# One transformer block on one core: gates and branch projections with features on partitions

## The chip, the cores and the metric

The kernel runs on one core of a Trainium2 chip, in one launch. The metric is device time in microseconds (us) from start to end of an execution. TensorE (PE) multiplies, VectorE (DVE) and ScalarE (ACT) do the elementwise work, GpSimd (POOL) does a little, and nearly all transfers from memory are issued by SyncE (SP).

## What is computed

One block of a hybrid model for 256 tokens of width 1024. The part that the change touches, cut from the reference:

```python
proj = jnp.einsum('bsd,de->bse', h, w_in[l])
qa, ka, va, qb, kb, vb, gate_logits = jnp.split(proj, splits, axis=-1)
oa = moba_attention(to_heads(qa, 8), to_heads(ka, 8), to_heads(va, 8), rel_bias)
ob = stick_breaking_attention(to_heads(qb, 8), to_heads(kb, 8), to_heads(vb, 8))
ya = jnp.einsum('bse,ed->bsd', merge_heads(oa), w_br_moba[l])     # 512 -> 1024
yb = jnp.einsum('bse,ed->bsd', merge_heads(ob), w_br_sb[l])       # 512 -> 1024
gates = jax.nn.sigmoid(gate_logits)
g_a, g_b = jnp.split(gates, 2, axis=-1)
mixed = jnp.einsum('bsd,de->bse', g_a * ya + g_b * yb, w_out[l])  # 1024 -> 1024
x = x + gt_m[:, None, :] * mixed
```

Ahead of it stand the modulation vectors and a norm, behind it a second norm, a gated feed-forward part with a short convolution (`up`, `down`) and the last norm.

## The kernel before

All products are made from two halves: a value is split into a rounded part (`wh`, `zh`, ..., a cast on ACT) and the rest (`wl`, `zl`, ..., a subtraction on DVE), and each product is three matmuls (high by high, low by high, high by low). `split` does this for weights, 1024 columns at a time, `hilo` for activations.

A `Stage` is one projection onto 512 output features. Its contraction is cut into units of two blocks of 128 rows. There are two ways to run a unit. In the token form (`Stream.mm`, line 164) 128 tokens are the stationary operand, 512 columns of weights move, and the output bank holds tokens on partitions; a unit is six matmuls of 128x512 for each of the two token tiles. In the feature form (`mm_fm`, line 252) 128 weight columns are the stationary operand, all 256 tokens move, and the output holds features on partitions; a unit is 24 matmuls of 128x256 in two halves. `qkb` and most of `up` use the feature form, the others the token form.

The order of stages is `gate0`, `gate1`, `qkb0`, `qkb2`, `vb`, `gate2`, `gate3`, then `ya0`, `ya1`, `yb0`, `yb1` (the branch projections), `out0`, `out1`, `up`, `down`. `together` runs a unit for both token tiles in turn; `staggered` runs token tile 1 some units behind token tile 0. While `gate0` to `ya1` run, generators add the attention of eight head pairs (`moba_pair`, then `stick_pair`; four pairs each) and the modulation vectors: `ada_part` loads pieces of 128x1024 into a pool of two buffers and accumulates them on DVE (`acc_gtm`, `acc_shf`, `acc_scf`, line 700). From these programs a scheduler with priorities makes one fixed sequence for each engine; each engine then goes through its sequence in order and waits at semaphores. PSUM banks of the stages come from a pool of three (`mm`), weight parts from pools of six (`wh`, `wl`), raw weights from a pool of three.

The gates: `gate_put` applies tanh to the bank (ACT, lines 759 to 764; for the second branch a copy first, and tanh in place when all heads are done) and keeps the result in an SBUF tile of 128x2048, tokens on partitions. `ya_put` multiplies one plus the gate by the bank (DVE, line 822). `yb_put` does the same for the second gate (line 829), adds (line 830), transposes the sum with four matmuls against the identity into a bank `zt` (line 838), and splits `zt` into `zh` and `zl` (lines 147, 148), the stationary operands of `out`. When the last of the four is made, the loads of `x` for the residual are issued (line 834).

## Time and profile before

| | us |
|---|---|
| median of 3 runs | 433.92 (433.38 to 434.75) |
| the profiled execution | 434.69 |
| its span, first to last instruction | 433.0 |
| PE busy | 410.1 (95%) |
| DVE busy | 335.6 (77%) |
| ACT busy | 254.0 (59%) |

The profile is of one execution. Times in it count from the start of the span. The mean granted TensorE clock was 0.982 of full speed. Matmuls overlap, so the pace of a stream of them is read from starts, not from the length of one.

### The profile page before, as it was taken

To read this page: it belongs to the slowest core of one execution; us is meant where nothing else is said; L and a number is where in the kernel's file an instruction comes from. 1 tells how busy PE (TensorE), PEld (TensorE's weight loads), DVE (VectorE), ACT (ScalarE), POOL (GpSimd) and SP (SyncE) were. 2 spreads that over 40 slices of the span, in tenths; PEclk is the share of its full clock that TensorE was granted. 3 is DMA by queue.
4 is the path that set the end of the run, shared out by engine and by line. 5 is a ranking of instruction groups with operands and counts; after the bars stand their busy time and mean duration, and the time that the engine had idled before them with its cause. 6 is when DMAs were issued, how large, how long until landed. Compare 5 with 4: busy or idle time off the path is not lost.

```text
span 433.0 us, 6769 instructions
## 1 busy us (share of the span) xinstructions
PE 410.1 (95%) x2598; PEld 364.4 (84%) x2598; DVE 335.6 (77%) x509; ACT 254.0 (59%) x397; POOL 41.4 (10%) x76
## 2 busy tenths in 40 slices
PE   7899889999799899999996999999999999999993
PEld 7898887789698688788884899999999999888882
DVE  3789969689689977996858779999998888546333
ACT  3244537867966779942446758666776666433312
POOL 3624430000001010000041000000000000000001
PEclk9999969999999999999999999999999999999997
DMA  8999987988467556577537487677576655473102
GB/s 260 323 325 332 290 287 259 323 292 289 147 239 254 188 203 234 197 244 288 177 115 242 155 277 251 202 254 247 178 226 175 183 193 195 149 266 122 47 0 97
DMA packets 67128, 94.44 MB, mean 218 GB/s; under 512 B 2558, under 2 KB 45697, under 8 KB 67096
## 3 DMA queue, kind: packets, MB, share of 16 engines
q1 hardware_dynamic: 65943, 90.77, 63.6%
q0 software_dynamic: 576, 1.67, 1.2%
q10 hardware_dynamic: 576, 1.57, 1.0%
q8 instruction: 20, 0.33, 0.3%
q14 instruction: 13, 0.10, 0.1%
HBM read 92.94 MB, written 1.06 MB: 217 GB/s over the span
## 4 chain that ended last, share of the span: by engine, by line
PE 61%; DVE 13%; ACT 9%; DMA 8%; issue 4%; SPq 1%; POOL 1%; POOLq 0%; DVEq 0%; ACTq 0%
PE ps_up L252 26%; PE ps_down L164 14%; DVE acc L385 4%; PE ps_out L164 4%; DMA ada_gtm<-in_w_ada_dram 3%; PE ps_yb L164 3%; PE ps_ya L164 3%; PE ps_qkb L252 3%; DMA raw_wA<-in_w_in_dram 2%; PE ps_up L164 2%; DMA ada<-in_w_ada_dram 2%; PE pA L406 1%; DMA ada_shf<-in_w_ada_dram 1%; DVE wl_gate L139 1%; SPq L365 1%
## 5 line engine op out<-in xcount | busy, mean ns | idle before, releaser
L138 ACT CAST wh_up<-raw_up 128x1024 fp32r<-128x1024 f32 x44 | 46.1, 1050 | 27.7 <-PE ps_up L252 21.9
L252 PE MATMUL ps_up<-h2h__2313,wh_up 128*128 128x256 f32 x320 | 58.0, 283 | 0.0
L252 PE MATMUL ps_up<-h2h__2313,wl_up 128*128 128x256 f32 x320 | 57.9, 283 | 0.0
L139 DVE TENSOR_TENSOR wl_up<-raw_up,wh_up 128x1024 fp32r<-128x1024 f32 x42 | 51.1, 1220 | 8.5 <-ACT wh_up L138 8.3
L252 PE MATMUL ps_up<-h2l__2314,wh_up 128*128 128x256 f32 x320 | 57.1, 279 | 0.0
L252 PEld LDWEIGHTS ps_up<-h2h__2313,wl_up 128*128 128x128 f32 x320 | 46.9, 191 | 0.0
L139 DVE TENSOR_TENSOR wl_down<-raw_down,wh_down 128x1024 fp32r<-128x1024 f32 x22 | 26.9, 1224 | 25.6 <-ACT wh_down L138 25.6
L252 PEld LDWEIGHTS ps_up<-h2l__2314,wh_up 128*128 128x128 f32 x320 | 46.6, 190 | 0.0
L252 PEld LDWEIGHTS ps_up<-h2h__2313,wh_up 128*128 128x128 f32 x320 | 46.4, 189 | 0.2
L138 ACT CAST wh_down<-raw_down 128x1024 fp32r<-128x1024 f32 x22 | 23.2, 1053 | 32.2 <-PE ps_down L164 23.6
L941 DVE SCALAR_TENSOR_TENSOR cv<-ps_up,wc,cv 128x255 f32<-128x255 f32 (+1 forms) x80 | 34.4, 476 | 1.4 <-ACT cv L935 0.9
L164 PE MATMUL ps_down<-wl_down,hh_a 128*128 128x512 f32 x88 | 34.9, 397 | 0.0
L164 PE MATMUL ps_down<-wh_down,hh_a 128*128 128x512 f32 x88 | 34.7, 395 | 0.0
L164 PE MATMUL ps_down<-wh_down,hl_a 128*128 128x512 f32 x88 | 34.7, 394 | 0.0
L164 PE MATMUL ps_gate<-wh_gate,hh 128*128 128x512 f32 x64 | 26.2, 409 | 1.9 <-DVE vbl L145 1.5
L385 DVE SCALAR_TENSOR_TENSOR acc<-ada,ca,acc 128x256 f32<-128x256 f32 (+1 forms) x43 | 24.7, 576 | 1.5
L164 PE MATMUL ps_gate<-wl_gate,hh 128*128 128x512 f32 x64 | 25.4, 396 | 0.0
L164 PE MATMUL ps_gate<-wh_gate,hl 128*128 128x512 f32 x64 | 25.3, 396 | 0.0
L935 ACT ACTIVATE cv<-ps_up,vc,wc 128x256 f32<-128x256 f32 x40 | 20.5, 562 | 5.7 <-PE ps_up L252 5.7
L139 DVE TENSOR_TENSOR wl_gate<-raw_gate,wh_gate 128x1024 fp32r<-128x1024 f32 x16 | 20.3, 1286 | 3.2 <-ACT wh_gate L138 3.2
L478 ACT CAST whA<-raw_wA 128x1024 fp32r<-128x1024 f32 (+1 forms) x9 | 8.6, 958 | 22.9 <-DMA raw_wA<-in_w_in_dram 22.9
L164 PEld LDWEIGHTS ps_down<-wh_down,hh_a 128*128 128x128 f32 x88 | 16.5, 188 | 4.1
(268 smaller groups left out, 930.7 us busy)
## 6 DMA issues: line engine op xcount, KB each, us to landing
raw_up<-in_w_up_dram SPq DMA_DIRECT2D x44, 512.0 KB, 5.0
raw_down<-in_w_down_dram SPq DMA_DIRECT2D x10, 1024.0 KB, 5.0
ada<-in_w_ada_dram SPq DMA_DIRECT2D x16, 512.0 KB, 7.5
raw_gate<-in_w_in_dram SPq DMA_DIRECT2D x8, 1024.0 KB, 7.2
raw_wA<-in_w_in_dram SPq DMA_DIRECT2D x8, 768.0 KB, 9.0
raw_qkb<-in_w_in_dram SPq DMA_DIRECT2D x8, 512.0 KB, 5.7
ada_gtm<-in_w_ada_dram SPq DMA_DIRECT2D x8, 512.0 KB, 5.4
ada_shf<-in_w_ada_dram SPq DMA_DIRECT2D x8, 512.0 KB, 5.7
```

Of the source, the lines that this page charges most:

```text
L138: nc.scalar.copy(wh[:, :n], t[:, a:a + n])
L139: (lo or nc.vector).tensor_sub(wl[:, :n], t[:, a:a + n], wh[:, :n].bitcast(F32))
L164: nc.tensor.matmul(ps, sx(k)[:, sl], w[:, c0:c0 + n], start=first and i == 0, stop=last and i == 2)
L252: nc.tensor.matmul(st.ps[f // 2][:, f % 2 * S:(f % 2 + 1) * S], wi[:, kk * 512 + f * P:kk * 512 + (f + 1) * P], sx(k0 + kk), start=first a ...
L365: nc.sync.dma_start(raw[:, i * D:(i + 1) * D].rearrange("p (k f) -> p k f", f=P), w_ada[:, i * D + j * P:i * D + (j + 1) * P].rearrange("( ...
L385: nc.vector.scalar_tensor_tensor(a, wk[:, parts, k, :], ca[:, k:k + 1], a, op0=ALU.mult, op1=ALU.add)
L406: nc.tensor.matmul(psqk[f // 2][:, f % 2 * S:(f % 2 + 1) * S], wp[0][n == 2][:, f * P:(f + 1) * P], (hh, hl, hh)[n][:, j, :], start=j == 0 ...
L478: nc.scalar.copy(wh[i][:, a:a + n], wws[j][:, i * 1024 + a:i * 1024 + a + n])
L935: nc.scalar.activation(ct[:, b, :], tp[:, b * S:(b + 1) * S], AF.Identity, bias=bconv[:, fb:fb + 1], scale=wc[:, 88 + fb:89 + fb])
L941: nc.vector.scalar_tensor_tensor(ct[:, b, d:], tp[:, b * S:(b + 1) * S - d], wc[:, (2 - d) * 44 + fb:(2 - d) * 44 + fb + 1], ct[:, b, d:], ...
```

## The change

The four gate stages and the four branch stages run in the feature form. The gate tiles therefore hold features on partitions, 8 blocks of 128 features by 256 tokens, and so do the products with the branch projections. Their sum has the layout that `zh` and `zl` need, so it is split straight from the gate tile in SBUF, and the 16 transposes and their banks are left out. `yb` runs `together`, and no longer staggered by six units. The loads of `x` are issued behind the `yb` stages.

```diff
+    def blocks(i, half):
+        return slice(4 * i + 2 * half, 4 * i + 2 * half + 2)
 ...
-                gates[g] = att.tile([P, NT, D], F32, tag=("ga", "gc")[g], name=f"gate{g}")
-            gt = gates[g][:, t, i % 2 * 512:(i % 2 + 1) * 512]
+                gates[g] = att.tile([P, KT, S], F32, tag=("ga", "gc")[g], name=f"gate{g}")
+            gt = gates[g][:, blocks(i % 2, half), :].rearrange("p a b -> p (a b)")
 ...
-        return Stage(f"gate{i}", KT, columns(w_in, GA + i * 512), tiles(hh), tiles(hl), gate_put(i))
+        return Stage(f"gate{i}", KT, columns(w_in, GA + i * 512), tiles(hh), tiles(hl), gate_put(i), fm=True)
 ...
+    def gated(g, i, half, ps):
+        gt = gates[g][:, blocks(i, half), :]
+        nc.vector.scalar_tensor_tensor(gt, gt, 1.0, ps.rearrange("p (a b) -> p a b", a=2), op0=ALU.add, op1=ALU.mult)
+        return gt
 ...
-            g0, g1 = (gates[g][:, t, i * 512:(i + 1) * 512] for g in range(2))
-            nc.vector.scalar_tensor_tensor(g1, g1, 1.0, ps, op0=ALU.add, op1=ALU.mult)
+            half, ps = ps
+            g1, g0 = gated(1, i, half, ps), gates[0][:, blocks(i, half), :]
             nc.vector.tensor_add(g0, g0, g1)
 ...
-                    nc.sync.dma_start(xr[tt], x[tt * P:(tt + 1) * P, :])
-            yield 3
-            tp = bank(sm, f"zt{t}{i}")
-            for a in range(4):
-                nc.tensor.transpose(tp[:, a * P:(a + 1) * P], g0[:, a * P:(a + 1) * P], ident)
-            s4 = slice(4 * i, 4 * i + 4)
-            tsl = slice(t * P, (t + 1) * P)
-            hilo(zh[:, s4, tsl], zl[:, s4, tsl], tp.rearrange("p (a b) -> p a b", a=4), 0.5)
+            hilo(zh[:, blocks(i, half), :], zl[:, blocks(i, half), :], g0, 0.5)
+            yield 1
 ...
-    staggered([u for us in y_units[2:] for u in us], 6)
+    together([u for us in y_units[2:] for u in us])
+    for t in range(NT):
+        nc.sync.dma_start(xr[t], x[t * P:(t + 1) * P, :])
```

The `ya` and `yb` stages get `fm=True` too. The scheduler also orders work around these stages in another way, at three places above all.

DVE during `gate1` and `qkb0` (stretch 97 to 108 us of the profile), before: `acc_gtm` are the pieces of a modulation vector, `wl_qkb` weight halves, `pl` the low half of the second head pair's probabilities, which the products `po_m` need.

```order
111 L700 SCALAR_TENSOR_TENSOR acc_gtm<-ada_gtm_1048,ca,acc_gtm 128x1024
112 L139 TENSOR_TENSOR wl_qkb_0_1195<-raw_qkb_0_969,wh_qkb_0_1194 128x1024
113 L616 RECIPROCAL su_1058<-su_1058 128x4
114 L139 TENSOR_TENSOR wl_qkb_2_1250<-raw_qkb_0_969,wh_qkb_2_1249 128x1024
115 L145 TENSOR_TENSOR oa_771<-po_m_1071,oa_770 64x256
116 L632 TENSOR_TENSOR pl_1101<-pt_1102,ph_1100 128x384
117 L632 TENSOR_TENSOR pl_1101<-pt_1107,ph_1100 128x384
118 L145 TENSOR_TENSOR oa_771<-po_m_1071,oa_770 64x256
119 L700 SCALAR_TENSOR_TENSOR acc_gtm<-ada_gtm_1129,ca,acc_gtm 128x1024
```

The same stretch of DVE now:

```order
111 L700 SCALAR_TENSOR_TENSOR acc_gtm<-ada_gtm_1138,ca,acc_gtm 128x1024
112 L700 SCALAR_TENSOR_TENSOR acc_gtm<-ada_gtm_1225,ca,acc_gtm 128x1024
113 L616 RECIPROCAL su_1148<-su_1148 128x4
114 L139 TENSOR_TENSOR wl_qkb_0_1291<-raw_qkb_0_1029,wh_qkb_0_1290 128x1024
115 L145 TENSOR_TENSOR oa_771<-po_m_1167,oa_770 64x256 x2
116 L700 SCALAR_TENSOR_TENSOR acc_gtm<-ada_gtm_1274,ca,acc_gtm 128x1024
117 L632 TENSOR_TENSOR pl_1197<-pt_1198,ph_1196 128x384
118 L632 TENSOR_TENSOR pl_1197<-pt_1203,ph_1196 128x384
119 L139 TENSOR_TENSOR wl_qkb_2_1346<-raw_qkb_0_1029,wh_qkb_2_1345 128x1024
```

The last two pieces of `acc_gtm`, which wait for transfers, moved ahead: one of them now stands directly in front of `pl`.

DVE at the start of `gate2` (stretch 135 to 144 us), before: `acc_shf` are pieces of the next modulation vector.

```order
157 L145 TENSOR_TENSOR qk_1477<-ps_qkb_1_1316,qk_1477 128x512
158 L139 TENSOR_TENSOR wl_gate_2_1629<-raw_gate_0_1346,wh_gate_2_1628 128x1024
159 L700 SCALAR_TENSOR_TENSOR acc_shf<-ada_shf_1558,ca,acc_shf 128x1024
160 L700 SCALAR_TENSOR_TENSOR acc_shf<-ada_shf_1602,ca,acc_shf 128x1024
161 L659 SCALAR_TENSOR_TENSOR t_1562<-zs_1530,t_1562 128x768
```

DVE at the start of `gate2` now:

```order
157 L145 TENSOR_TENSOR qk_1573<-ps_qkb_1_1412,qk_1573 128x512
158 L700 SCALAR_TENSOR_TENSOR acc_shf<-ada_shf_1654,ca,acc_shf 128x1024
159 L139 TENSOR_TENSOR wl_gate_2_1725<-raw_gate_0_1442,wh_gate_2_1724 128x1024
160 L700 SCALAR_TENSOR_TENSOR acc_shf<-ada_shf_1698,ca,acc_shf 128x1024
161 L659 SCALAR_TENSOR_TENSOR t_1658<-zs_1626,t_1658 128x768
```

One piece of `acc_shf` moved ahead of a weight half; the last transfer for that vector is issued when this piece is done.

DVE at the end of `yb` (stretch 197 to 210 us), before:

```order
222 L830 TENSOR_TENSOR gate_905<-gate_905,gate_1807 128x512
223 L829 SCALAR_TENSOR_TENSOR gate_1807<-gate_1807,ps_yb_0_2100 128x512
224 L830 TENSOR_TENSOR gate_905<-gate_905,gate_1807 128x512
225 L139 TENSOR_TENSOR wl_out_4_2170<-raw_out_4_2043,wh_out_4_2169 128x1024
226 L148 SCALAR_TENSOR_TENSOR zl<-zt_2128,zh 128x4x128
227 L829 SCALAR_TENSOR_TENSOR gate_1807<-gate_1807,ps_yb_1_2121 128x512
228 L139 TENSOR_TENSOR wl_out_6_2188<-raw_out_4_2043,wh_out_6_2187 128x1024
```

DVE at the end of `yb` now:

```order
224 L826 SCALAR_TENSOR_TENSOR gate_1945<-gate_1945,ps_yb_1_2317 128x512
225 L139 TENSOR_TENSOR wl_out_6_2463<-raw_out_4_2271,wh_out_6_2462 128x1024
226 L148 SCALAR_TENSOR_TENSOR zl<-gate_947,zh 128x512
227 L839 TENSOR_TENSOR gate_947<-gate_947,gate_1945 128x512
228 L139 TENSOR_TENSOR wl_out_0_2476<-raw_out_0_2345,wh_out_0_2475 128x1024
229 L148 SCALAR_TENSOR_TENSOR zl<-gate_947,zh 128x512
230 L826 SCALAR_TENSOR_TENSOR gate_1945<-gate_1945,ps_yb_0_2385 128x512
231 L826 SCALAR_TENSOR_TENSOR gate_1945<-gate_1945,ps_yb_1_2398 128x512
232 L839 TENSOR_TENSOR gate_947<-gate_947,gate_1945 128x512 x2
233 L139 TENSOR_TENSOR wl_out_2_2486<-raw_out_0_2345,wh_out_2_2485 128x1024
234 L148 SCALAR_TENSOR_TENSOR zl<-gate_947,zh 128x512 x2
```

The last two sums (row 232) come behind two weight halves of `out`, and the last two `zl` behind a third.

## Rows read from the trace of the kernel before

**Rows 1.** The page, part 1: busy us (share of the span), instructions.

```profile
PE 410.1 (95%) x2598; PEld 364.4 (84%) x2598; DVE 335.6 (77%) x509; ACT 254.0 (59%) x397; POOL 41.4 (10%) x76
```

**Rows 2.** Waits of PE, 60 to 250 us: total us, times, longest.

```profile
PE ps_qkb L252 <- DVE qk L148: 2.4, 1, 2.4
PE ps_gate L164 <- DVE vbl L145: 1.5, 1, 1.5
PE cu L668 <- DVE lkl L663: 1.0, 1, 1.0
```

**Rows 3.** Stretches (us): busy (instructions) of PE, PEld, DVE, ACT, POOL; clock; DMA.

```profile
98.00:110.00 12.00, 12.00 (x105) 11.68 (x104) 11.16 (x22) 8.82 (x25) 0.00 (x0) 1.00 0.78 260
110.00:123.00 13.00, 10.61 (x67) 8.84 (x68) 9.26 (x14) 9.84 (x18) 0.00 (x0) 0.87 0.49 162
160.00:175.00 15.00, 14.04 (x70) 11.58 (x70) 12.17 (x16) 13.68 (x20) 1.05 (x2) 1.00 0.52 176
193.00:207.00 14.00, 14.00 (x74) 11.72 (x73) 10.52 (x16) 5.31 (x6) 0.54 (x1) 1.00 0.64 227
```

**Rows 4.** The chain that ended last: start us, us, what.

```profile
180.92 5.60 PE ps_ya L164 x24
205.18 0.44 PE zt L838 x4
260.29 54.22 PE ps_up L252 x456
```

**Rows 5.** PE in order of time: start us, us, what, and idle before.

```profile
104.47 0.39 PE L575 MATMUL po_m<-ph,vah 128*128 128x512 f32 x1
116.10 0.51 PE L252 MATMUL ps_qkb<-hh,wh_qkb 128*128 128x256 f32 x2 [2.39 <-DVE qk L148]
```

**Rows 6.** DVE in order of time, 101 to 145 us, same columns.

```profile
101.51 1.00 DVE L632 TENSOR_TENSOR pl<-pt,ph 128x384 fp32r<-128x384 f32 x2
103.00 1.28 DVE L700 SCALAR_TENSOR_TENSOR acc_gtm<-ada_gtm,ca,acc_gtm 128x1024 f32<-128x1024 f32 x1
107.75 0.16 DVE L611 TENSOR_SCALAR mx<-mx 128x4 f32<-128x4 f32 x1
114.22 1.22 DVE L139 TENSOR_TENSOR wl_vb<-raw_vb,wh_vb 128x1024 fp32r<-128x1024 f32 x1 [0.59 <-ACT wh_vb L138]
115.36 0.68 DVE L148 SCALAR_TENSOR_TENSOR qk<-ps_qkb,qk 128x512 fp32r<-128x512 f32 x1
144.13 1.28 DVE L700 SCALAR_TENSOR_TENSOR acc_shf<-ada_shf,ca,acc_shf 128x1024 f32<-128x1024 f32 x1 [0.43 <-DMA ada_shf<-in_w_ada_dram]
```

**Rows 7.** ACT in order of time, 107 to 115 us.

```profile
107.95 0.51 ACT L614 ACTIVATE sb<-sb,mx 128x256 f32<-128x256 f32 x1 [3.11 <-DVE mx L611]
114.08 0.61 ACT L147 ACTIVATE qk<-ps_qkb 128x512 fp32r<-128x512 f32 x1
```

**Rows 8.** SP's queue in order of time, and the landing of `ada_gtm` transfers.

```profile
94.91 3.48 SPq L706 DMA_DIRECT2D ada_gtm<-in_w_ada_dram  x2
...
DMA to landing us min/median/max: 4.7/5.4/6.0
```

**Rows 9.** One of the stretches after the wait at 113.7: PE busy, clock, DMA.

```profile
118.00:119.00 1.00, 1.00 (x5) 0.50 0.00 0
```

**Rows 10.** ACT and DVE at the end of `yb`, in order of time.

```profile
201.99 1.05 ACT L138 CAST wh_out<-raw_out 128x1024 fp32r<-128x1024 f32 x1 [7.72 <-PE ps_yb L164]
...
204.82 0.68 DVE L829 SCALAR_TENSOR_TENSOR gate<-gate,ps_yb 128x512 f32<-128x512 f32 x1
205.41 1.22 DVE L139 TENSOR_TENSOR wl_out<-raw_out,wh_out 128x1024 fp32r<-128x1024 f32 x1
206.55 0.68 DVE L830 TENSOR_TENSOR gate<-gate,gate 128x512 f32<-128x512 f32 x1
```

**Rows 11.** Groups by line, 55 to 250 us: busy us, mean ns.

```profile
L148 DVE SCALAR_TENSOR_TENSOR zl<-zt,zh 128x512 fp32r<-128x512 f32 x4 | 2.7, 686 | 0.9 <-ACT zh L147 0.9
L145 DVE TENSOR_TENSOR h2l__2314<-h2f,h2h__2313 128x512 fp32r<-128x512 f32 x4 | 2.7, 688 | 0.4 <-ACT h2h__2313 L144 0.3
```

More of the change, by code (lines that the diff above doesn't have):

```diff
@@ L817, in block_kernel @@
     zl = slot("hl", [P, KT, S], F32R, "zl")
+    def gated(g, i, half, ps):
+        gt = gates[g][:, blocks(i, half), :]
+        nc.vector.scalar_tensor_tensor(gt, gt, 1.0, ps.rearrange("p (a b) -> p a b", a=2), op0=ALU.add, op1=ALU.mult)
+        return gt
     def ya_put(i):
         def put(t, ps):
-            g = gates[0][:, t, i * 512:(i + 1) * 512]
-            nc.vector.scalar_tensor_tensor(g, g, 1.0, ps, op0=ALU.add, op1=ALU.mult)
-            yield 3
+            gated(0, i, *ps)
+            yield 1
         return put
@@ L827, in put @@
         def put(t, ps):
-            g0, g1 = (gates[g][:, t, i * 512:(i + 1) * 512] for g in range(2))
-            nc.vector.scalar_tensor_tensor(g1, g1, 1.0, ps, op0=ALU.add, op1=ALU.mult)
+            half, ps = ps
+            g1, g0 = gated(1, i, half, ps), gates[0][:, blocks(i, half), :]
             nc.vector.tensor_add(g0, g0, g1)
-            if i == 1 and t == 1:
+            if i == 0 and half == 0:
                 for tt in range(NT):
                     xr[tt] = slot(f"x{tt}", [P, D], F32, f"xr{tt}")
-                    nc.sync.dma_start(xr[tt], x[tt * P:(tt + 1) * P, :])
-            yield 3
-            tp = bank(sm, f"zt{t}{i}")
-            for a in range(4):
-                nc.tensor.transpose(tp[:, a * P:(a + 1) * P], g0[:, a * P:(a + 1) * P], ident)
-            s4 = slice(4 * i, 4 * i + 4)
-            tsl = slice(t * P, (t + 1) * P)
-            hilo(zh[:, s4, tsl], zl[:, s4, tsl], tp.rearrange("p (a b) -> p a b", a=4), 0.5)
+            hilo(zh[:, blocks(i, half), :], zl[:, blocks(i, half), :], g0, 0.5)
+            yield 1
         return put
@@ L895, in h2_at @@
         return lambda k: h2[i][:, k, :]
-    y_units = [stream.add(Stage(f"ya{i}", NHP, columns(w_br_moba, i * 512), tiles(oah), tiles(oal), ya_put(i)))
+    y_units = [stream.add(Stage(f"ya{i}", NHP, columns(w_br_moba, i * 512), tiles(oah), tiles(oal), ya_put(i), fm=True))
                for i in range(2)]
-    y_units += [stream.add(Stage(f"yb{i}", NHP, columns(w_br_sb, i * 512), tiles(obh), tiles(obl), yb_put(i)))
+    y_units += [stream.add(Stage(f"yb{i}", NHP, columns(w_br_sb, i * 512), tiles(obh), tiles(obl), yb_put(i), fm=True))
                 for i in range(2)]
```

## The prediction

> **What bounds the kernel now.** I began with the page's first part: PE is busy for 95% of the span [rows 1], so only time on PE, or a wait of PE, can matter. Next, the waits of PE from the gates to the second norm: the three that lie where the change works sum to about 5 us, 2.4 for a PSUM bank that DVE frees by writing `qk`, 1.5 for `vbl`, 1.0 for `lkl` [rows 2]. Each hangs on DVE or ACT, not on PE itself. The stretches then sort the stages. From 98 to 110 us, and from 193 to 207 us, where `ya` and `yb` run, PE is busy throughout; from 110 to 123 and from 160 to 175 us it is not [rows 3]. So an edit on PE's own work counts in full in the branch projections, and is paid out of a wait in the gates. The chain of waits agrees: from `ya` to the end of `out` it runs on PE almost alone, the transposes among it [rows 4].
>
> **The change part by part.** *The feature form on PE.* It does 288 matmuls of 512 columns (48 for each of four gate stages, 24 for each of four branch stages) as 576 of 256 columns. The chain gives the pace of both: 24 of the long kind in 5.60 us, 233 ns each; 456 of the short kind in 54.22 us, 118.9 ns each [rows 4]. 24 long ones cost 5.60, and 48 short ones 5.71, so each group of 24 becomes 0.11 us dearer: 0.43 us for `gate0` and `gate1`, 0.43 for `gate2` and `gate3`, 0.43 for `ya` and `yb`, 1.3 us in all.
>
> [...]
>
> *The transposes.* Four groups of four, 0.44 us each [rows 4], lie on a PE that never waits there: 4 x 0.44 = 1.76 us go.
>
> *Branch stages.* +0.43 - 1.76 = -1.33 us at the end of `out`, if `zh` and `zl` come in time.
>
> *First gates.* PE is full up to 113.7 us, so their 0.43 us delays it, but then it waits 2.39 us, up to 116.10 [rows 5], for the bank that DVE's `qk` frees. The 0.43 us is free as long as that moment stands still. It need not. In the new order of DVE, the last `acc_gtm` piece stands in front of `pl`. Its transfer needs a buffer that the piece before the last but one frees; SP is done with the second of the two issues of 94.91 at 98.4, so it gives it out at about 98.0, and landing takes 5.4 us (4.7 to 6.0) [rows 8]. So DVE can do this piece at 103.4 (102.7 to 104.0) and not before; the piece is 1.28 us, `pl` comes behind it, at about 104.6 instead of 101.51 [rows 6], and is done at about 105.6. PE wants `pl` at 104.47 plus 0.43 [rows 5]: a new wait of about 0.7 us, covered by the wait at 113.7. More weighty: ACT's softmax of the last pair waits for `mx`, now at 107.75 [rows 6, 7]. The work in front of `mx` is the same, so it comes later by what DVE stands still: from none to the 2.5 us between 101.5 and 104.0; I take 1.3, about the middle. From there ACT takes 6.1 us to `qk` (107.95 to 114.08) [rows 7], the same casts in another order; DVE then loses less, since `wl_vb` (1.22 us) no longer ends so late against `qk` [rows 6], which gives back about 0.6. The bank comes at about +0.7 us (-0.5 to +2.1).
>
> *Carry to 175 us.* From 116 us on PE is full again until it waits for `vbl` and `lkl`, and both end when DVE and ACT say. In the new order one `acc_shf` piece passes a weight half of about 1.2 us, so the last transfer of that vector is issued earlier, and DVE's wait of 0.43 us for it [rows 6] can go. I take 0.5 us of the 0.7 as swallowed there and by the slack in DVE: +0.2 us at 175 us, with -0.9 (the low end, with the transfer's wait gone as well) and +2.1 (all of it carried) as bounds. The 0.43 us of `gate2` and `gate3` goes into the wait of 1.0 us for `lkl` [rows 2], but for the last 16 long matmuls, which come behind it: +0.07.
>
> *`zh` and `zl`.* No row of before shows this split from SBUF. The nearest pair is `zl` from PSUM, 686 ns, against `h2l` from SBUF, 688 [rows 11]: no difference, and I use the old durations. On DVE the pace is 0.59 us for 512 columns and 1.14 for 1024 (from 204.82, 205.41 and 206.55) [rows 10]. Let E be the end of `yb` on PE. From E - 5.7, when the second bank of `yb0` is done, DVE does in order one product, a weight half, `zl`, a sum, a weight half, `zl`, two products and a sum: 7 x 0.59 + 2 x 1.14 = 6.4 us, with some 0.6 us of waits for casts on ACT. So the third sum is there at about E + 1.3 to 2.0 and its cast, taken as long as one such operation, 0.6 us later, at E + 1.9 to 2.7. `out` needs it after two units, 12 x 0.233 = E + 2.8. The new order even puts a unit of the second token tile in between before it needs `zl`. I take 0.1 us of wait, between 0 and 1.2 (two more operations on DVE). The cast that waited 7.72 us for `yb` to free its buffer [rows 10] can start earlier, as `together` frees buffers one unit at a time.
>
> [...]
>
> *The rest.* The transfers of `x` keep their place in SP's queue, between the last loads for `out`, and the residual needs them only when `out` has its first bank: nothing. The gate's ACT and DVE operations are as many and as large as before: nothing.
>
> **Sum.** -1.33 + 0.07 + 0.2 + 0.1 = -0.96 us, say -1.0. The profiled execution took 434.69 us, so it becomes 433.7; the median of the runs is 433.92, 0.77 lower, and becomes **432.9 us**.
>
> **The rivals.** *The front gains as well* (2 in 10). If the `acc_gtm` transfers land early, the bank comes at -0.5, and the `acc_shf` swap takes 0.4 more. [...] For it: a smaller stall is enough. Against it: the new queue at `acc_gtm`. Time: 433.92 - 1.33 + 0.07 + 0.1 - 0.9 = 431.9, and down to 431.2 with part of the clock.
>
> *The queue at `acc_gtm` decides* (1.5 in 10), slower than before. One mechanism: `pl`, and the last pair's scores behind it, wait for a transfer. It decides from the point where the transfer lands 2.3 us behind the moment at which DVE is ready for it, for SP has 1 MB of `raw_vb` to fetch next to it. Price: `mx` 2.1 us late, the bank with it, and the 0.5 us of slack not there: -1.26 + 0.1 + 2.1 = +0.9, 434.9 us; 435.3 with the bound of the casts on ACT. For it: SP's wait and DVE's in one chain. Against it: DVE has weight halves to do first.
>
> *`zh` late* (1 in 10). `out` stands for the bound of 1.2 us: -0.96 + 1.1 = +0.1, 434.1 us, no change.
>
> The forecast has 5.5 in 10, with 432.2 to 433.7 as its own range.
>
> **How the numbers follow.** A measurement of this kernel can tell about 0.3% from no change, 1.3 us: below 432.6 or above 435.2. Faster: 0.18 of the forecast's 0.55 lies below 432.6, and nearly all of the first rival: 0.38. Slower: 0.06 of the queue's case, 0.01 of late `zh`, and 0.05 for what I have not seen in an order that changed on three engines: 0.12. The rest, 0.50, is within. The range that leaves out 2 in 10 goes from 431.4 (into the first rival) to 435.0 (past the queue's price).
>
> **What would show it.** In the profile of the changed kernel: no `zt`; `ps_ya` in the chain at about 5.7 us for 48; PE's waits: `qk` still there, at about 2 us, ending near 116.8, a wait of `po_m` for `pl` of under 1 us at 105; `ps_out` following `ps_yb` with no wait of PE over 0.3 us. A wait of PE for `zh` over 1 us, a short pace far from 119 ns, or a bank for `qkb` that comes over 2 us late or at all earlier would make the prediction wrong, each with its own sign.

## The result: slower by 1.4%

| | before | after |
|---|---|---|
| median of 6 runs, us | 434.38 (433.38 to 434.84) | 440.40 (439.23 to 442.15) |
| ratio after/before, 95% interval | | 1.0144 (1.0118 to 1.0170) |
| profiled execution, us | 434.69 | 440.63 |
| its span, us | 433.0 | 438.9 |

The forecast was 432.9 us with a range up to 435.0; the time lies 5.4 us above the range. To find the place, I set the starts of the same work on PE side by side in the two traces.

| start on PE, us | before | after | after is late by |
|---|---|---|---|
| first `ps_gate` | 68.48 | 67.92 | -0.56 |
| first `ps_qkb` | 95.67 | 96.84 | +1.17 |
| `ps_qkb` behind the wait for `qk` | 116.10 | 118.05 | +1.95 |
| first `z` | 122.40 | 122.81 | +0.41 |
| second group of `z` | 131.60 | 131.95 | +0.35 |
| third group of `z` (inside `vb`) | 139.64 | 144.38 | **+4.74** |
| `ps_gate` behind the wait for `vbl` | 149.01 | 153.52 | +4.51 |
| `cu` behind the wait for `lkl` | 174.75 | 179.16 | +4.41 |
| first `ps_ya` | 180.76 | 185.72 | +4.96 |
| first `ps_out` | 206.86 | 212.78 | +5.92 |
| first `ps_up` | 234.38 | 239.57 | +5.19 |
| second `h2t` | 238.05 | 244.02 | +5.97 |

PE was level at 132 us, lost 4.4 us up to the third group of `z`, and from `ya` on nothing came back. The waits of PE in the changed kernel (same view as [rows 2]; its columns are total us, times, longest):

```profile
PE ps_vb L164 <- DVE qk L148: 2.6, 1, 2.6
...
PE ps_qkb L252 <- DVE qk L148: 2.3, 1, 2.3
...
PE ps_gate L252 <- DVE vbl L145: 1.3, 1, 1.3
PE cu L668 <- DVE lkl L663: 1.1, 1, 1.1
PE ps_yb L252 <- DVE gate L826: 0.9, 1, 0.9
PE po_m L575 <- DVE pl L632: 0.7, 1, 0.7
```

The three waits of [rows 2] are still there, about as long. Three are new: `ps_vb` for the second `qk`, `ps_yb` for a bank, and `po_m` for `pl`. (The wait for `ka` in front of the first `ps_gate`, ahead of what the change touches, is 1.58 us here and was 0.35.) DVE in order of time (as [rows 6]; the bracket is the idle time in front and what ended it) shows where the first of these comes from:

```profile
104.27 1.28 DVE L700 SCALAR_TENSOR_TENSOR acc_gtm<-ada_gtm,ca,acc_gtm 128x1024 f32<-128x1024 f32 x1 [2.47 <-DMA ada_gtm<-in_w_ada_dram]
105.59 1.02 DVE L632 TENSOR_TENSOR pl<-pt,ph 128x384 fp32r<-128x384 f32 x2
...
109.90 0.15 DVE L611 TENSOR_SCALAR mx<-mx 128x4 f32<-128x4 f32 x1
...
117.30 0.69 DVE L148 SCALAR_TENSOR_TENSOR qk<-ps_qkb,qk 128x512 fp32r<-128x512 f32 x1
...
129.32 2.60 DVE L700 SCALAR_TENSOR_TENSOR acc_shf<-ada_shf,ca,acc_shf 128x1024 f32<-128x1024 f32 x2 [2.54 <-DMA ada_shf<-in_w_ada_dram]
...
136.30 0.68 DVE L148 SCALAR_TENSOR_TENSOR qk<-ps_qkb,qk 128x512 fp32r<-128x512 f32 x1
...
148.65 1.28 DVE L700 SCALAR_TENSOR_TENSOR acc_shf<-ada_shf,ca,acc_shf 128x1024 f32<-128x1024 f32 x1 [1.56 <-DMA ada_shf<-in_w_ada_dram]
...
152.78 0.68 DVE L145 TENSOR_TENSOR vbl<-ps_vb,vbh 128x512 fp32r<-128x512 f32 x1
```

DVE stands still three times for over 1 us for a piece of a modulation vector: 2.47 us for the last `acc_gtm` piece, 2.54 for the third `acc_shf` piece, and 1.56 for the last one, where it was 0.43 [rows 6]. Behind the second stall stand, in DVE's fixed order, two pieces, `wl_vb`, `t`, another piece, `lkl`, and only then the `qk` row at 136.30, whose bank PE wants at 134.44. Behind the third stall DVE is busy without a break up to `vbl` at 152.78, for which PE waits next. PE in order of time, and two stretches (columns as in [rows 3]: the last three are granted clock, DMA share, GB/s):

```profile
137.04 0.67 PE L164 MATMUL ps_vb<-wh_vb,hh 128*128 128x512 f32 x1 [2.60 <-DVE qk L148]
...
201.07 0.50 PE L252 MATMUL ps_yb<-ob,wh_yb 128*128 128x256 f32 x2 [0.89 <-DVE gate L826]
...
239.57 0.78 PE L164 MATMUL ps_up<-wh_up,h2h__2581 128*128 128x512 f32 x1 [2.28 <-ACT h2h__2581 L144]
```

```profile
118.00:123.00 5.00, 4.95 (x38) 4.65 (x40) 4.43 (x6) 4.28 (x7) 0.00 (x0) 1.00 0.22 62
137.00:142.00 5.00, 4.96 (x15) 3.92 (x16) 4.94 (x6) 3.12 (x5) 1.75 (x2) 0.66 0.62 251
239.00:244.00 5.00, 4.43 (x12) 3.45 (x13) 4.44 (x10) 1.65 (x5) 1.00 (x2) 0.66 0.77 267
```

Behind the 2.60 us the clock was 0.66 on average from 137 to 142 us: 24 `ps_vb` took 7.4 us (137.04 to 144.45), 1.8 more than the 5.6 of [rows 4]. That makes the +4.74, but it is not what makes `ya` late (see the step that failed). Behind the 2.27 us at 118.05 it stayed at 1.00, where in the kernel before it had fallen to 0.50 [rows 9] (0.66 from 116 to 121 us); that is why the +1.95 of the bank is +0.41 at the first `z`. Behind the 2.28 us at 239.57 it fell to 0.66 (239 to 244 us), which costs the last 0.8 us of the table.

### The profile page after: what moved, and what is told of

Read it like the earlier page. It is cut to its first block, busy times and chain, and to the rows that moved or that the text cites. A ratio compares the mean times of both kernels' runs of the same rounds, so it can differ in the third digit from the quotient of the medians.

```text
span 438.9 us, 7308 instructions
## 1 busy us (share of the span) xinstructions
PE 412.0 (94%) x2870; PEld 379.4 (86%) x2870; DVE 336.0 (77%) x509; ACT 253.8 (58%) x397; POOL 40.1 (9%) x76
## 4 chain that ended last, share of the span: by engine, by line
PE 57%; DMA 14%; DVE 14%; ACT 8%; issue 5%; POOL 1%; SPq 1%; POOLq 0%; DVEq 0%; ACTq 0%
PE ps_up L252 26%; PE ps_down L164 14%; DMA ada_gtm<-in_w_ada_dram 4%; DMA ada_shf<-in_w_ada_dram 4%; PE ps_out L164 4%; DMA ada<-in_w_ada_dram 3%; PE ps_up L164 3%; DVE acc L385 3%; PE ps_yb L252 2%; PE pA L406 2%; PE ps_gate L252 2%; DMA ada_scf<-in_w_ada_dram 2%; DMA raw_gate<-in_w_in_dram 2%; PE pV L411 1%; DVE wl_gate L139 1%
## 5 line engine op out<-in xcount | busy, mean ns | idle before, releaser
L252 PEld LDWEIGHTS ps_up<-h2h__2581,wl_up 128*128 128x128 f32 x320 | 46.9, 191 | 0.0
L252 PE MATMUL ps_gate<-hh,wh_gate 128*128 128x256 f32 x128 | 24.4, 293 | 2.9 <-DVE ka L145 1.6
L252 PE MATMUL ps_gate<-hh,wl_gate 128*128 128x256 f32 x128 | 23.6, 287 | 0.0
L252 PE MATMUL ps_gate<-hl,wh_gate 128*128 128x256 f32 x128 | 23.5, 286 | 0.0
L252 PEld LDWEIGHTS ps_gate<-hh,wh_gate 128*128 128x128 f32 x128 | 19.1, 194 | 3.6 <-DVE ka L145 1.8
```

What stands on the lines that cost most here:

```text
L252: nc.tensor.matmul(st.ps[f // 2][:, f % 2 * S:(f % 2 + 1) * S], wi[:, kk * 512 + f * P:kk * 512 + (f + 1) * P], sx(k0 + kk), start=first a ...
```

## The experiments

The theory: the loss is made by the place of the modulation pieces in DVE's order and by the transfers that they wait for, not by the feature form. The rivals: the feature form is dear by itself; the second stall has its own cause. The scheduler plans the whole kernel anew in each run, so an edit can also move instructions that it does not name; where the traces show this, it is said. All medians below stand against 434.3 to 434.5 us of the kernel before on the same chip.

**e1_pin.** `pin` keeps an instruction behind all that was written before it on its engine.

```diff
-                nc.vector.scalar_tensor_tensor(acc, w[k], ca[:, k:k + 1], acc, op0=ALU.mult, op1=ALU.add)
+                i_ = nc.vector.scalar_tensor_tensor(acc, w[k], ca[:, k:k + 1], acc, op0=ALU.mult, op1=ALU.add)
+                if nm == "gtm" and k > 5:
+                    pin(i_)
...
-            nc.vector.tensor_sub(lo, back, hi.bitcast(F32))
+            i_ = nc.vector.tensor_sub(lo, back, hi.bitcast(F32))
+            if hp == 1:
+                pin(i_)
```

> The changed kernel, with only the last two pieces of `acc_gtm` kept behind `pl` of the second head pair on DVE, as they stood before; everything in feature form. Theory (the order of DVE against the transfers): the wait of DVE for the last `acc_gtm` piece in front of `pl` (2.47 us) is gone, `qk` frees the bank near 116.5, the `ada_shf` transfers are issued some 2 us earlier, PE's wait of 2.60 us for `qk` at 134 falls under 0.5 us, `ya` starts near 181.5 instead of 185.7: 436.0 us (435.0 to 437.0). Rival (the feature form itself is dear in the gates, by its pace or by the clock): the front stays as long, 440 us (439 to 441).

Measured: 436.45 us, ratio 1.0048 (1.0026 to 1.0070). The 2.47 us are gone, `ya` starts at 181.36, and of the waits for `qk` this is left:

```profile
PE ps_vb L164 <- DVE qk L148: 1.1, 1, 1.1
PE ps_qkb L252 <- DVE qk L148: 1.0, 1, 1.0
```

The order of DVE put back there, with every matmul still in feature form, gives 4 of the 6 us back. It is not the two instructions alone: in this trace the `acc_shf` piece at the start of `gate2` is behind its weight half again too, as in the kernel before, and DVE's wait for the last piece is 0.68 us and not 1.56.

**e2_pieces4.** `ob` (the slots `xn0`, `xn1`) is made when the second branch's first head writes it.

```diff
-            w.append(adap.tile([P, D], F32, tag="ada", name=f"ada_{nm}{k}"))
+            if nm in ("gtm", "shf") and k % 4 > 1:
+                w.append(slot(f"xn{k % 4 - 2}", [P, D], F32, f"ada_{nm}{k}"))
+            else:
+                w.append(adap.tile([P, D], F32, tag="ada", name=f"ada_{nm}{k}"))
```

> The changed kernel, with four buffers in place of two for the pieces of the first two modulation vectors (two lie in space that is idle until the second branch's heads are done). The order of DVE up to 140 us stays as in the changed kernel, the last `acc_gtm` piece in front of `pl`; only the transfers start earlier. Theory (DVE stands still for transfers): DVE's waits for `ada_gtm` and `ada_shf` between 96 and 135 us, 6.2 us in all, fall under 1 us, PE's wait of 2.60 us at 134 is gone: 435.5 us (434.0 to 437.0). Rival one (the piece of 1.28 us in front of `pl` costs by its own length, wherever its data are): most of the loss stays, 438.5 us (437.5 to 439.5). Rival two (the feature form is dear): 440 us.

Measured: 435.18 us, ratio 1.0020 (0.9997 to 1.0042). DVE's two stalls in its trace, the answers to 104.27 and 129.32 above:

```profile
100.86 1.28 DVE L700 SCALAR_TENSOR_TENSOR acc_gtm<-ada_gtm,ca,acc_gtm 128x1024 f32<-128x1024 f32 x1 [0.19 <-DMA ada_gtm<-in_w_ada_dram]
...
125.72 1.29 DVE L700 SCALAR_TENSOR_TENSOR acc_shf<-ada_shf,ca,acc_shf 128x1024 f32<-128x1024 f32 x1 [0.29 <-DMA ada_shf<-in_w_ada_dram]
```

The second and third `acc_shf` pieces, from 118.66 on, and the last, at 142.17, do not wait at all; a wait of 2.36 us for an earlier `ada_gtm` piece, ending at 95.53, is left. With the `acc_gtm` pieces where the change put them and the transfers earlier, 5.2 us come back, so the piece's own 1.28 us in front of `pl` is not the bulk of the loss. From 118 us on the order is another one, though: five pieces still stand in front of the second `qk`, but in other places, and the swap at the start of `gate2` is undone.

**e4_before_early.** The start table begins with 1, not 3, in the kernel before.

```diff
-    spawn(modulation([3 + int(2.5 * i) for i in range(3 * KT)]))
+    spawn(modulation([1 + int(2.5 * i) for i in range(3 * KT)]))
```

> The kernel before, all in the token form, with the modulation vectors started two events earlier, which puts the last two pieces of `acc_gtm` in front of `pl` of the second head pair on DVE, as the change did. Theory (that place in the order costs, whatever form the matmuls have): DVE stands still in front of `pl` for the transfer, by 1 to 2.5 us, the bank of `qk` comes 1 to 2 us late, PE gets a new wait near 133 us: 437.0 us (435.5 to 439.0). Rival (only together with the feature form, which makes PE late as well, does it cost): 434.4 us (433.8 to 435.0), as before; if the earlier start brings the transfers forward as well, also that.

Measured: 437.74 us, ratio 1.0075 (1.0051 to 1.0098): the token form loses 3.4 us by another order alone. Its profiled execution (435.3 us) is the fastest of its ten, so its trace doesn't show the loss, only the times do. In that trace DVE does not stand still in front of `pl`, which the theory said it would, so that this loss has the same cause is not shown.

**e5_before_pieces4.** The edit of e2_pieces4 on the kernel before.

> The kernel before, all in token form, with four buffers in place of two for the pieces of the first two modulation vectors, as in the run e2_pieces4 of the changed kernel. Theory (in the kernel before the transfers were hidden, but for a small part: DVE waits 6.6 us for them between 70 and 150 us, mostly beside waits for ACT, and the bank of `qk` comes late for other reasons): 433.9 us, a gain of 0.5 (433.0 to 434.6), so that the four buffers are worth ten times as much to the changed kernel, which lost its order, as to this. Rival (the waits for transfers bound both alike): 430.0 us, and the changed kernel is then 5 us behind it still.

Measured: 433.70 us, ratio 0.9980 (0.9958 to 1.0002): 0.8 us, not clear of noise, against 5.2 for the changed kernel.

**e9_gtm4, e10_shf4.** Four buffers for one of the two vectors.

```diff
-            if nm in ("gtm", "shf") and k % 4 > 1:
+            if nm == "gtm" and k % 4 > 1:
```

> The changed kernel with four buffers for the pieces of `acc_gtm` alone; those of `acc_shf` have two, as in the changed kernel, and the order of DVE is that of the changed kernel. Theory (the loss begins at the last `acc_gtm` piece; the late `ada_shf` transfers and PE's wait of 2.60 us behind it are its consequence, since SP issues these transfers when DVE has come through): with the first stall gone the second goes too, 436.0 us (435.2 to 437.0), most of the 5.2 us between the changed kernel and the run e2_pieces4. Rival (the `ada_shf` transfers are late for their own reason, two buffers and a queue): only some 2 us come back, 438.4 us (437.6 to 439.2).

> The changed kernel with four buffers for the pieces of `acc_shf` alone; those of `acc_gtm` have two, as in the changed kernel. Theory: the first stall stays, `qk` frees the first bank near 118, but two of the `ada_shf` pieces are on their way before DVE asks for them, so the wait of 2.54 us at 126.8 falls under 1 us and the shift does not grow from 2 us to 4.4: 438.0 us (437.0 to 439.0). Rival (the second stall is the whole loss): 435.5 us; other rival (the shift of 2 us alone makes the second bank late, whatever the transfers do, and the clock falls behind it): 440 us.

Measured: 437.73 us (ratio 1.0078, 1.0051 to 1.0105) and 436.19 (1.0043, 1.0020 to 1.0066). Here the theory had it wrong: alone the first vector's buffers give 2.7 us, the second's 4.2, together 5.2. The trace of e9_gtm4, DVE and then PE in order of time:

```profile
113.08 0.69 DVE L148 SCALAR_TENSOR_TENSOR qk<-ps_qkb,qk 128x512 fp32r<-128x512 f32 x1
...
125.09 2.60 DVE L700 SCALAR_TENSOR_TENSOR acc_shf<-ada_shf,ca,acc_shf 128x1024 f32<-128x1024 f32 x2 [2.52 <-DMA ada_shf<-in_w_ada_dram]
```

```profile
132.96 0.50 PE L164 MATMUL ps_vb<-wh_vb,hh 128*128 128x512 f32 x1 [2.78 <-DVE qk L148]
```

DVE's order here is that of the changed kernel all through the front, so this is the cleanest of the runs with four buffers. Counted from the first `ps_gate`, the first `qk` comes at 46.2 us, against 46.9 in the kernel before and 49.4 in the changed one, and yet the stall at `acc_shf` with PE's wait behind it is as long as in the changed kernel, and so is the one for the last piece (1.54 us). So the later stalls are no echo of the first: DVE releases those transfers itself. From the moment at which SP issues the third `ada_shf` piece DVE needs 4.7 us to come to it, in the kernel before, the changed one and e9_gtm4 alike, and what the landing takes beyond that (5.8, 7.2 and 7.1 us) it waits, however early it is. In e10_shf4 the order changed as in e2_pieces4, so its 4.2 us are buffers and order together.

**e15_shf_late.** The same, by order: only the second and third vector start four events later.

```diff
-    spawn(modulation([3 + int(2.5 * i) for i in range(3 * KT)]))
+    spawn(modulation([3 + int(2.5 * i) + (4 if i >= KT else 0) for i in range(3 * KT)]))
```

> The changed kernel with only the second and third modulation vectors started four events later. On DVE the last `acc_gtm` piece still stands in front of `pl`, four `acc_shf` pieces instead of five stand in front of the second `qk`, but a `wl_gate` half has come in front of it too. Theory (the transfers that DVE itself releases are the second stall): with one piece less the second `qk` comes about 1 us sooner, the rest of the loss stays: 439.0 us (438.0 to 440.2). Rival (the shift of 2 us from the first stall is what counts, and the pieces behind it only pass it on): 440.4 us. Other rival (the fifth piece, whose transfer is released last, is the second stall): 436.5 us.

Measured: 439.12 us, ratio 1.0099 (1.0075 to 1.0123): the time is the theory's, but the trace doesn't show that the piece made it, since the third transfer took only 5.6 us there. PE's wait at `ps_vb` fell from 2.60 to 0.19 us, but the one for `vbl` rose to 3.5: two of the pieces now stand in front of that.

**e3_fourbanks, e7_pieces4_bank.** The fourth bank for `yb`, first by the count as it stood (`stream.four = True` alone), then so that `yb0` begins with it (on top of e2_pieces4).

```diff
+    stream.four, stream.banks = True, 3
     together([u for us in y_units[2:] for u in us])
```

> The changed kernel, with the fourth PSUM bank, which lies idle once the heads are done, given to the stages from `yb` on and not only from `out` on. Theory: of the 1.16 us that PE waits for banks freed by `ya`'s products (0.27 and 0.89) the longer goes, and from the start of `yb` to the start of `out` it takes 0.9 us less: 439.5 us (439.0 to 440.0). Rival (the branch stages lost their gain to the pace of the short matmuls, and DVE is late with the products anyway, so the wait moves to the next bank): no change, 440.4 us (440.0 to 440.8).

> The changed kernel with four buffers for the modulation pieces, and with the fourth PSUM bank given to the first half of `yb0` (the run e3_fourbanks gave it to the fourth half, by the count of the rotation, and so left the wait where it was). Theory: `yb0` begins on a bank that nobody holds, the wait of 0.86 us for the product of `ya1` is gone, and from the start of `ya` to the start of `out` it takes 25.9 us in place of 26.8: 434.3 us against 435.2 of the run e2_pieces4 (433.6 to 434.8). Rival (the wait moves on to the next half, since DVE is as late with the next product): 435.2 us.

Measured: 441.24 us for e3_fourbanks, with the 0.89 us where it was: the rotation reached the free bank only at the fourth half, a fault of my edit. e7_pieces4_bank: 433.70 us, ratio 0.9984 (0.9967 to 1.0001); no wait of PE in `yb`, and 25.60 us from `ya` to `out`.

**e6_no_transposes.** `hilo(zh, zl, ...)` reads the sum in the gate tile, and `zt` with its four transposes is cut, in the kernel before. `out` then multiplies a matrix that is not transposed; the run times one part of the change alone.

```diff
-            tp = bank(sm, f"zt{t}{i}")
-            for a in range(4):
-                nc.tensor.transpose(tp[:, a * P:(a + 1) * P], g0[:, a * P:(a + 1) * P], ident)
...
-            hilo(zh[:, s4, tsl], zl[:, s4, tsl], tp.rearrange("p (a b) -> p a b", a=4), 0.5)
+            hilo(zh[:, s4, tsl], zl[:, s4, tsl], g0.rearrange("p (a b) -> p a b", a=4), 0.5)
```

> The kernel before in token form, with the 16 transposes of the gated sum left out: `zh` and `zl` are split from the sum as it lies, tokens on partitions, so the products of `out` are of the wrong matrix. It has the time of the one part of the change that takes work off PE. The prediction's term: four groups of 0.44 us, so from the start of `ya` to the start of `up` it takes 1.76 us less than the 53.62 of before. Rival (a group costs PE 0.355 us, the distance from its start to the start of what follows, as the matmuls overlap): 1.42 us less. In both cases 432.6 to 433.0 us. A third way (`zh` is late without the bank `zt`, and `out` waits): no gain, 434.4 us.

Measured: 433.09 us, ratio 0.9959 (0.9936 to 0.9981). PE where `ya`, `out` and `up` start:

```profile
180.15 0.39 PE L164 MATMUL ps_ya<-wh_ya,oa 128*128 128x512 f32 x1
...
205.38 0.40 PE L164 MATMUL ps_out<-wh_out,zh 128*128 128x512 f32 x1
...
231.97 0.50 PE L164 MATMUL ps_up<-wh_up,h2h__2293 128*128 128x512 f32 x1 [2.28 <-ACT h2h__2293 L144]
```

From `ya` to `up` it takes 51.82 us, 1.80 less than the 53.62 of before: the term of 1.76 was right.

**e8_pieces4_pin_bank.** e7_pieces4_bank with the edit of e1_pin.

> The run e7_pieces4_bank with the last two pieces of `acc_gtm` also kept behind `pl`. Theory (the pieces cost twice, by the transfer and by their own 1.28 us each in front of `pl`; the four buffers take away the first, the place in the order the second): `qk` frees its bank about 1.3 us sooner than in e7_pieces4_bank, of which the later waits for `qk` and `vbl` take back half: 433.7 us (432.8 to 434.6). Rival (with the transfers early enough, PE's waits behind are set by ACT and by the heads, not by these pieces): the same as e7_pieces4_bank, 434.3 us.

Measured: 433.97 us, ratio 0.9992 (0.9971 to 1.0014): the rival. The wait for the first `qk` fell from 1.65 to 0.54 us, the ones for the second `qk` (0.89) and `vbl` (1.84) stayed.

**e11_pool, e12_before_pool, e13_late_bank, e14_before_late.** Two attempts to relieve DVE in front of what PE waits for, each in both forms: five weight halves to GpSimd (below; on top of e7_pieces4_bank and of e5_before_pieces4), and a start table that begins with 7 (with two buffers, the feature form with the bank).

```diff
-    stream.on_pool = up_units[0][0:2]
+    stream.on_pool = [*up_units[0][0:2], units[0][2], units[4][0], units[5][0], units[5][3], units[6][0]]
```

> The run e7_pieces4_bank, with five weight halves that stand on DVE just in front of what PE waits for (`ka`, twice `qk`, twice `vbl`) done by GpSimd, which is idle there. Theory (with the transfers out of the way, PE's waits of 1.92, 1.65, 0.74 and 1.86 us in e7_pieces4_bank are DVE's queue of weight halves): they fall by 1 to 1.2 us each where a half is gone, 3 to 4 us in all, of which the wait for `lkl` (ACT and DVE in turn) takes back about 1: 431.0 us (429.5 to 432.5), faster than both kernels. Rival (the waits end on ACT, whose casts are as many, or DVE slows down beside GpSimd): 433.7 us (433.2 to 434.5).

> The run e5_before_pieces4 (token form) with the same five weight halves on GpSimd as in e11_pool. Theory: the same 2 to 3 us come off, 431.0 us (429.5 to 432.5), so that the two forms stand level in the same surroundings, as e5_before_pieces4 and e7_pieces4_bank did (433.7 both). Rival (the feature form's gain of 1.2 us in the branch stages shows once the front no longer waits): e11_pool is 1 us or more faster than this one.

> The changed kernel with the modulation vectors started four events later (two buffers, as in the changed kernel) and the fourth bank given to the first half of `yb0`. On DVE `pl` now stands in front of the last two `acc_gtm` pieces, only the first two `acc_shf` pieces stand in front of the second `qk`, and the first `wl_vb` and `wl_gate` halves stand behind the `qk` rows that free a bank. Theory (the place of the pieces in DVE's order made the loss, the transfers only its size): both stalls are gone, PE's waits for `qk` fall under 1.5 and 0.5 us, 433.0 us (432.0 to 434.2), level with e7_pieces4_bank or better. Rival (the pieces that come later make the vectors late, and a wait takes their place at `gate2`, `vbl` or the sums `ps_shf`): 436 us.

> The kernel before, in token form, with the modulation vectors started four events later: the same order of DVE between the second head pair and the end of the second `qkb` stage as in e13_late_bank. Theory (the two forms are level: 1.2 us gained in the branch stages, 1.0 to 1.4 lost in the gates, of which 0.5 is the wait for `lkl` that falls between other units): the same time as e13_late_bank within 0.8 us, 433.0 us. Rival (the form itself gains, as predicted, and only the order hid it): this one is 1.0 to 1.5 us slower than e13_late_bank, 434.3 us. Other rival (the form itself loses): this one is 1.5 us faster, 431.5 us.

Measured: 438.73, 436.69, 442.64 and 440.30 us; all four came out 6 to 10 us above what I expected (the rivals on record were at most 436). The first fence is DVE in order of time in e11_pool, where the first `qk` now waits for ACT; the second is PE's waits in e13_late_bank:

```profile
116.60 0.69 DVE L148 SCALAR_TENSOR_TENSOR qk<-ps_qkb,qk 128x512 fp32r<-128x512 f32 x1 [1.27 <-ACT qk L147]
```

```profile
PE ps_gate L252 <- DVE vbl L145: 4.4, 1, 4.4
PE ps_qkb L252 <- DVE qk L148: 3.7, 1, 3.7
```

What leaves one place of DVE's queue comes in front of another wait of PE, or lays ACT bare. They answer the question of the form, though, with e2, e5 and e7:

| surroundings | token form | feature form |
|---|---|---|
| four buffers | 433.70 (e5) | 435.18 (e2), with the bank 433.70 (e7) |
| the same, five halves on GpSimd | 436.69 (e12) | with the bank 438.73 (e11) |
| vectors four events later | 440.30 (e14) | with the bank 442.64 (e13) |

The feature form gains in none. It is 1.5, 2.0 and 2.3 us slower in e2, e11 and e13, and level only in e7, where (as in e11 and e13) it has a bank more than its partner. Of the cases on record for e14_before_late the one in which the form itself loses comes nearest. So the theory holds for most of the 6 us, not for all: what is left lies with the form or with the orders that come with it, and no run separates these. From `ya` to `up` its traces are 1.2 to 1.4 us shorter than their partners (52.39 in e7, 52.36 in e11, 52.24 in e13, against 53.6), but `ya` starts later: by 1.4 us in e2 against e5, 1.5 in e11 against e12, 2.6 in e13 against e14 (one trace each). No version that computes the right product beats the kernel before beyond its interval.

## Why the prediction was wrong, step by step

*What bounds the kernel.* Right, but read too kindly: PE is 95% busy [rows 1], but each of its waits from 98 to 175 us ends when DVE or ACT says, and I took the time between them for PE's own. Two other orders of the same kernel are 3.4 us (e4) and 5.8 us (e14) slower.

*Price of the feature form.* Right where nothing waits: 0.37 us from `ya` to `out` (e7 against e6), predicted 0.43.

*The transposes.* Right: 1.80 (e6), predicted 1.76.

*Branch stages, -1.33.* Wrong by a wait that I did not look for: 53.85 us from `ya` to `up`, +0.23. `staggered` had run all four `yb` units of token tile 0 between the first bank of `yb0` and the second; `together` asks for both within one unit, while `ya1` still holds two of three banks. 0.27 + 0.89 us of waits follow; the bank of e7 takes them away and leaves 52.39, which is -1.23. (In e15 PE doesn't wait there either, with three banks; why was not followed up.) I asked only whether `zh` is in time, not whether a bank is. `zh` itself cost nothing, as the wait for `ps_out` that I allowed did not come.

*First gates' 0.43 us, hidden.* Not shown, and probably not. e2 and e5, whose waits for the bank end at 114.63 and 114.24, don't answer it, since the piece in front of `pl` differs between them too. But e2 and e7 have one order up to `ya`, and in e7 the clock fell behind the wait for `ka` (0.66 over 5 us, 1.00 in e2; two short matmuls 0.43 us and not 0.24). PE's wait for the bank in e2, then in e7:

```profile
114.63 0.51 PE L252 MATMUL ps_qkb<-hh,wh_qkb 128*128 128x256 f32 x2 [1.77 <-DVE qk L148]
```

```profile
116.62 0.51 PE L252 MATMUL ps_qkb<-hh,wh_qkb 128*128 128x256 f32 x2 [1.65 <-DVE qk L148]
```

From the first `ps_gate` to the first `ps_qkb` it takes 27.43 us in e2 and 29.02 in e7, 1.59 more. The wait shrank by 0.12 us only, and its end moved from 47.22 to 48.69 us behind the first `ps_gate`, by 1.47. A wait covers added work only if its end does not depend on that work; the `qk` chain begins with scores that PE issues between the gate units (this last is argued, not measured alone). The changed kernel's first gates lost time to the clock in the same way (28.92 us, against 27.19 before).

*The bank at +0.7 (-0.5 to +2.1).* The mechanism and the place were right: the piece in front of `pl`, and PE's wait of 0.68 us for `pl` (predicted 0.7). That these agree is luck: PE came at 105.98 and not at 104.9, since the clock had fallen in `gate0` (0.66 from 67.92 to 72.92 us, 1.00 over the same 5 us in the kernel before), and `pl` was done at 106.6 and not at 105.6. The size was at the upper end: the transfer landed 6.2 us after its issue (bounds 4.7 to 6.0), DVE stood still 2.47 us and not 1.3, and the bank came 1.95 late. Three traces with one order up to there, after, e3 and e10, bear the mechanism out: landing took 6.2, 4.9 and 3.9 us, DVE stood still 2.47, 1.09 and 0.15 us, and the bank came 50.1, 49.1 and 48.0 us behind the first `ps_gate` (47.6 in the kernel before).

*Carry to 175 us, +0.2 (-0.9 to +2.1).* **This step failed**: +4.41. I called DVE's idle time behind the bank slack, swallowed 0.5 us in it, and let DVE's wait of 0.43 us for the last `acc_shf` piece go. Both were waits for transfers that DVE itself releases, and in both the delay grew.

The first: SP issues the third `ada_shf` piece when DVE has done the first (119.97 in the kernel before, 122.07 now), so every delay of DVE passes into it whole. On top, this transfer took 7.2 us to land, not 5.8, which makes +3.4 at the second `qk`. PE had about 0.3 us to spare there (bank free at 133.6, the matmul that wants it at 133.95), so a new wait of 2.60 us came, and the clock fell behind it.

The second: I had the last `ada_shf` piece issued when the piece that moved ahead is done, as the text on the change says. It is not. SP's queue has a `raw_gate` transfer in front of it, and that waits for the weight half which now stands behind the moved piece. The chain of work that ended last in the changed kernel (as [rows 4]) goes this way, while in the kernel before SP gave out the same two transfers at 137.47 and 138.82:

```profile
122.07 7.17 DMA ada_shf<-in_w_ada_dram
...
139.54 1.20 DVE acc_shf L700
140.76 1.43 DVE wl_gate L139
142.21 0.38 SPq L311
142.68 5.87 DMA ada_shf<-in_w_ada_dram
```

So the transfer was issued 3.9 us late and not early, DVE waited 1.56 us for it and not 0, and `vbl` came at 152.78 instead of 148.27: +4.5. The largest bound of the sum, +2.1, was the delay that goes in; nothing in it allowed for growth.

PE's wait of 2.60 us and the slow clock behind it are not on that chain. Without them PE would have stood longer at `vbl`: in e3, with the same order, the third `ada_shf` piece landed after 5.6 us, PE waited only 0.26 us at `ps_vb`, and then this long:

```profile
153.50 0.79 PE L252 MATMUL ps_gate<-hh,wh_gate 128*128 128x256 f32 x2 [4.12 <-DVE vbl L145]
```

That is 85.1 us behind the first `ps_gate`, against 85.6 in the changed kernel and 80.5 in the kernel before. There the last transfer took 7.1 us, and DVE waited 3.22 us for it. How long a landing takes differed from one execution to the next; that it decides here did not: from DVE's start on the last piece to PE's start behind `vbl` it takes 4.9 us in the kernel before, the changed one and e3 alike.

*`gate2` and `gate3`, +0.07.* +0.55. Ahead of the wait for `lkl` PE had done 20 of the last 36 long matmuls before, but now only 36 of 72 short ones, since the split falls between units: from that wait's end to `ya` it takes 6.56 us and not 6.01. I had the split where it was.

*The clock.* I gave it a price only as a gain. No run shows the 0.7 us that the first rival's 431.2 takes from the clock; what the runs showed is that the way from the wait for the bank to the first `z` took 4.76 us in the changed kernel, at 1.00 behind that wait, and 6.30 in the kernel before, at 0.66. What it cost in `gate0` was covered by DVE's first stall (SP issues the last `ada_gtm` piece 30.1 us behind the first `ps_gate`, and in e3, where PE kept its pace there, 0.24 us for two short matmuls and not 0.43, 30.3), and what it cost at `ps_vb` by the wait for `vbl`. Behind the wait for `h2h` in front of `up`, which is as long before (2.26 us) as after (2.28), it fell this time (0.66, against 1.00 before) and nothing covers it: +0.8. It is not the form's: it fell in e6, in token form (0.66), and not in e8 (1.00).

The terms as measured, 4.41 + 0.55 + 0.23 + 0.78, give 5.97 us; the spans differ by 5.9. The rival that named the first stall, the queue at `acc_gtm`, stopped at the bank, and so cost it at +0.9.

## What to carry to other kernels

Idle time in front of an operation whose transfer the same engine releases need not be slack: here, with two buffers, the delay went round the loop, engine to queue to transfer to engine, and came out undiminished (2.1 us at the issue of the third `ada_shf` piece, 3.4 at the second `qk`, with a landing 1.4 longer); more buffers gave 5.2 us to the kernel whose order was just disturbed, and 0.8 to the other. The last `ada_shf` transfer was not issued when its buffer was free (140.7 us), but when SP's queue came to it (142.68), so look at what stands in front of a transfer in its queue and what that waits for. And a wait that a trace shows is worth only what the next wait behind it doesn't take back (e8: 1.1 us less at the first `qk`, no gain in time). Where a change moves instructions, follow each moved one to the next thing that the bounding engine waits for behind it, and not only to the first. And a switch from a staggered to a joint order of tiles must be checked for banks as well as for operands.

## What the runs showed of the hardware

- *Landing times vary by place and execution.* The same transfer of 0.5 MB for the last `acc_gtm` piece landed 6.2, 4.9 and 3.9 us after its issue in the traces of after, e3 and e10, all with the same order up to there. The third `ada_shf` piece took 7.2 us in after, 7.1 in e9 and 5.6 in e3, in the same order too. In after the DMA share fell from 0.77 to 0.06 for the last 0.8 us of it, while DVE waited:

```profile
127.50:128.50 1.00, 1.00 (x11) 1.00 (x10) 0.00 (x0) 1.00 (x2) 0.00 (x0) 1.00 0.77 311
128.50:129.30 0.80, 0.80 (x9) 0.80 (x9) 0.00 (x0) 0.80 (x2) 0.00 (x0) 1.00 0.06 26
```

  The view gives only the mean over the 16 DMA engines; 0.06 is what one of them at work would give. A packet of the instruction queue (0.02 MB) lies in the stretch from the issue of this piece to its landing in after, e9 and e3, and none in the kernel before; but e3's landing was not late, so what held the end of this one back stays open.
- *The clock falls behind waits of equal length in some executions and not in others.* Behind 2.26 to 2.28 us in front of `up` the granted clock stayed at 1.00 in the kernel before and in e8, and was 0.66 over the 5 us behind in after and in e6 (token form). Behind the wait for `ka` in front of the first `ps_gate` it was 0.66 after 1.56 us (e6) and 1.92 us (e7), and 1.00 after 1.60 us (e5) and 2.03 us (e14). In these traces it follows neither the form nor the length of the wait.
- *Less work on DVE made both forms slower.* With five weight halves on GpSimd (2.3 to 3.3 us each there, 1.2 on DVE) the token form lost 3.0 us (e12 against e5) and the feature form 5.0 (e11 against e7). PE's wait for `vbl` rose from 1.84 to 3.33 us in e12 and from 1.86 to 3.32 in e11, and the one for the first `qk` from 1.54 to 2.28 and from 1.65 to 3.66. In e11 the first `qk` waits 1.27 us for ACT, which it did not before. What is in front of `vbl` shows why that came late: next to the halves on GpSimd DVE's own operations took longer. GpSimd and DVE in e12:

```profile
142.96 5.81 POOL L139 TENSOR_TENSOR wl_gate<-raw_gate,wh_gate 128x1024 fp32r<-128x1024 f32 x2 [4.60 <-ACT wh_gate L138]
```

```profile
143.18 3.37 DVE L700 SCALAR_TENSOR_TENSOR acc_shf<-ada_shf,ca,acc_shf 128x1024 f32<-128x1024 f32 x1
...
147.40 2.18 DVE L663 TENSOR_TENSOR lkl<-t,lkh 128x768 fp32r<-128x768 f32 x1
```

  The first takes 1.28 us and the second 0.95 in e5 (and in the kernel before), where GpSimd does none of these halves; in e11 they take 3.21 and 2.18. That is the rival on record for e11_pool, DVE slowing down beside GpSimd, at a higher price than it was given.
